# Layer 1's experts: first two gathered by one-hot products, norm's scale and shift on the transposed rows, sixteen weight buffers instead of twelve

## The chip, the core and the metric

The kernel runs on one core of a Trainium2 chip. A core has five engines, each with its own queue of instructions that it works off in the order in which they stand: TensorE (PE in the profile: matrix products, transposes too), VectorE (DVE), ScalarE (ACT), GpSimd (POOL) and SyncE (SP, which here only issues DMAs). Sixteen DMA engines move data between the device's memory and the core's on-chip memory. The metric is the device time of one execution in microseconds (us); less is better.

## The reference

Two layers (`DEPTH = 2`) of a block with four mixers and a mixture of experts run over 256 tokens and, in layer 0, 256 context tokens, each with 1024 numbers. The change concerns the mixture of experts of layer 1 and the norm ahead of it:

```python
def rms_norm(x, g):
    y = x * lax.rsqrt(jnp.mean(x * x, axis=-1, keepdims=True) + EPS)
    return y * g
def modulate(h, shift, scale):
    return h * (1.0 + scale) + shift
...
        x = x + gt1 * (jnp.concatenate([ya, yb, ys, yh], axis=-1) @ w_out[l])
        h2 = modulate(rms_norm(x, norm2_g[l]), sh2, sc2)
        x = x + gt2 * moe(h2, router_w, router_b, moe_w1[l], moe_w3[l], moe_w2[l])
...
def moe(h, w_router, b_router, w1, w3, w2):
    scores = jax.nn.softmax(h @ w_router + b_router, axis=-1)
    # the best of 4 groups of 4 experts, and in it the best 2 experts, with weights that sum to 1
    ...
    for e in range(16):
        he = jax.nn.silu(h @ w1[e]) * (h @ w3[e])
        out = out + gate[..., e:e + 1] * (he @ w2[e])
```

All is in 32-bit floating point. One expert's three matrices have 6 MB, sixteen experts' 96 MB, and each is read once in a layer.

## The kernel before

**The experts.** Routing gives each token's two choices a place in one of the experts' lists. In layer 1 an expert has a list of 64 rows, two of them 128 and 96. What does not fit goes to a loop of extra passes (`extras`, its count `rnx` is computed on the chip; in the run profiled here layer 1 makes no pass). Routing also sorts the experts from the third on by how many tokens they have, so which weights belong to the third, fourth, ... expert is known on the chip alone: `wix` holds the indices, SP reads one into a register (`wdyn`) and issues the loads of that expert's weights (`raw<-in_wmoe_dram`, six of 1 MB each). The first two experts (`STAT = 2`) are fixed, so their loads wait for no routing.

**The norm.** `norm` writes the normed, scaled and shifted rows of each of the two tiles of 128 tokens to a scratch tensor in memory, `h2d`; scale and shift (`a2`, `sh`) are broadcast by DMA to all partitions. GpSimd gathers an expert's rows from it (`xg<-h2d`), PE transposes them (`tp<-cst,xg`), and ACT copies the transposed rows out of the accumulator memory (`ah<-tp`).

**Routing's two halves.** `route` is a generator; its first part gives `p`, the place of each token in each expert's list. `first_slots` turns `p` into the row numbers of the first two experts (`oh`, `rsrc`) and issues their gathers. Then the other parts make `wix`, `rnx` and `rri`, by which GpSimd scatters each token's number and weight into a table in memory (`sld<-rec,rri`, four DMAs) and reads the table back (`rtab<-sld`). From `rtab` come the rows of all later gathers, the weights by which an expert's result is multiplied (`yf<-s,rtab`) and the rows to which it is added (`ybd<-yf,rtab`, a DMA that adds).

**One expert** (`expert32`): products with `w1` and `w3` (both `sc<-raw,ah`, in two accumulators), copies of both by ACT and DVE (`al<-sc`), products with a folding matrix (`tp<-fold,al`), silu on ACT (`al<-tp`), the product on DVE (`ah<-al,tp`), products with `w2` (`mm<-raw,ah`), then `s<-mm`, `s<-s,mm` and `yf<-s,rtab` for each half of the columns. `moe` writes the steps of neighbouring experts interleaved; a scheduler orders each engine's queue when the kernel is built.

**The weights' buffers.** `fetch` puts the 1 MB loads in turn into 12 buffers (7 + 3 + 2), in the order `USE`. A load waits for its buffer's last reader and for the load three ahead of it to have landed (`FLIGHT = 3`). Ahead of the loop over extra passes, which stands between experts 1 and 2, loads are issued until `AHEAD2` of them stand ahead of their use: 21 in all. At the loop each engine waits for every transfer under way.

## Time and profile before

| | |
|---|---|
| median of three runs | 1307.47 us (1305.84 to 1308.94) |
| profiled execution, its own time | 1307.14 us |
| its span, first to last instruction | 1305.1 us, 2.0 us less than its time |
| mean clock granted to TensorE | 0.931 of full speed |
| PE busy | 1146.0 us, 88% of the span |
| DVE, ACT, POOL busy | 731.1, 529.9, 183.9 us |
| loop over extra passes of layer 1 | PE waits for it from 1032.5 to 1042.0 us |

Times in the trace count from the first instruction. Layer 1's experts begin at some 984 us and end at some 1282 us. Since the sum of the busy times mixes stages with different limits, the stage between the norm and the loop has to be read by itself: when each engine works there, and what ends its waits.

### The profile page before, as it was taken

Reading aid. Unit: us, or ns where it says so; the run is one execution under the profiler, and the core shown is the slowest. Engines: PE = TensorE matmul, PEld = TensorE weight load, DVE = VectorE, ACT = ScalarE, POOL = GpSimd, SP = SyncE. Lnnn points to the kernel's source line nnn. Section 1 sums busy time; section 2 is a strip of 40 time slices with the busy share of each in tenths; the row PEclk is TensorE's granted clock in tenths of the full one; section 3 lists DMA queues with packets and bytes.
Section 4 is the critical chain, followed back from the end, with each engine's and each line's share of the span. In section 5 each row is a group of like instructions: output and inputs, shape, how many; then the busy total and the mean of one; then the engine's idle time right before and its main releaser. Section 6 shows DMA issues by size and latency. Waiting matters only on the chain. (4 is left out here: it accounts for less than half of the span.)

```text
span 1305.1 us, 16882 instructions
## 1 busy us (share of the span) xinstructions
PE 1146.0 (88%) x5789; PEld 724.5 (56%) x5789; DVE 731.1 (56%) x1811; ACT 529.9 (41%) x876; POOL 183.9 (14%) x213
## 2 busy tenths in 40 slices
PE   4999999997966799999898799998884499998885
PEld 2677677765855567655454277684771253533332
DVE  6496579788588564455444659599974110101114
ACT  5222642674324464555434452553831122212222
POOL 0200200100044220211100100100102111211102
PEclk9999999896987799999999899999896789999997
DMA  7763752444817798899995743554477699999961
GB/s 298 261 235 135 257 204 86 177 153 158 350 49 258 238 355 319 313 367 387 384 361 183 279 162 131 201 173 162 149 277 314 242 337 396 365 389 388 414 265 65
DMA packets 62009, 334.05 MB, mean 256 GB/s; under 512 B 12217, under 2 KB 13657, under 8 KB 27104
## 3 DMA queue, kind: packets, MB, share of 16 engines
q1 hardware_dynamic: 51840, 313.44, 63.0%
q0 software_dynamic: 10080, 19.50, 5.8%
q8 instruction: 47, 0.77, 0.2%
q14 instruction: 42, 0.34, 0.1%
HBM read 317.51 MB, written 19.15 MB: 258 GB/s over the span
## 5 line engine op out<-in xcount | busy, mean ns | idle before, releaser
L383 DVE TENSOR_TENSOR lo<-raw,hi 128x1024 fp32r<-128x1024 f32 x169 | 203.5, 1222 | 87.4 <-ACT hi L383 82.9
L383 PE MATMUL sc<-raw,ah 128*64 128x512 f32 (+3 forms) x750 | 216.2, 634 | 12.8 <-SPq L2031 9.5
L383 ACT CAST hi<-raw 128x1024 fp32r<-128x1024 f32 x172 | 175.3, 1047 | 116.5 <-PE mm L383 53.6
L383 PEld LDWEIGHTS sc<-raw,ah 128*64 128x64 f32 (+3 forms) x750 | 62.3, 147 | 113.3 <-issue 99.5
L383 PE MATMUL mm<-hi,ah 128*128 128x512 f32 (+3 forms) x264 | 109.1, 415 | 4.4 <-ACT hi L383 4.3
L383 PE MATMUL mm<-lo,ah 128*128 128x512 f32 (+3 forms) x264 | 107.0, 405 | 1.7 <-DVE lo L383 1.6
L383 PE MATMUL mm<-hi,al 128*128 128x512 f32 (+3 forms) x264 | 105.7, 402 | 0.6 <-DVE al L383 0.6
L383 PE MATMUL mm<-raw,ah 128*64 128x512 f32 (+3 forms) x378 | 100.2, 595 | 1.9 <-DVE ah L383 1.9
L383 PE MATMUL mm<-ah,hi 128*128 128x512 f32 (+1 forms) x224 | 88.4, 399 | 1.1 <-DVE ah L383 0.8
L383 PE MATMUL sc<-hi,ah 128*128 128x512 f32 (+3 forms) x176 | 75.8, 432 | 11.5 <-ACT hi L383 6.8
L383 DVE COPY al<-sc 128x512 f32<-128x512 f32 x21 | 14.5, 690 | 126.8 <-PE sc L383 126.8
L383 PE MATMUL mm<-al,hi 128*128 128x512 f32 (+1 forms) x224 | 83.8, 374 | 0.0
L383 PE MATMUL mm<-ah,lo 128*128 128x512 f32 (+1 forms) x224 | 83.2, 372 | 0.0
L383 PE MATMUL ad<-raw,cT 128*32 128x256 f32 (+1 forms) x512 | 67.7, 530 | 11.3 <-DMA raw<-in_wada_dram 8.5
L383 DVE TENSOR_TENSOR s<-s,mm 64x512 f32<-64x512 f32 (+1 forms) x43 | 29.2, 678 | 85.1 <-ACT s L383 85.1
L383 PE MATMUL sc<-lo,ah 128*128 128x512 f32 (+3 forms) x176 | 73.2, 416 | 2.1 <-DVE lo L383 2.1
L383 PE MATMUL sc<-hi,al 128*128 128x512 f32 (+3 forms) x176 | 72.1, 410 | 0.0
L383 PEld LDWEIGHTS tp<-fold,al 128*128 128x128 f32 x336 | 43.0, 201 | 48.9 <-DVE al L383 23.9
L383 PE MATMUL tp<-fold,al 128*128 128x64 f32 x336 | 46.9, 289 | 23.8 <-DVE al L383 14.9
L383 PEld LDWEIGHTS mm<-hi,ah 128*128 128x128 f32 (+3 forms) x264 | 49.4, 188 | 28.3 <-ACT hi L383 6.4
L383 PEld LDWEIGHTS mm<-raw,ah 128*64 128x64 f32 (+3 forms) x378 | 32.7, 142 | 58.3 <-issue 52.0
L383 ACT ACTIVATE al<-tp 128x256 f32<-128x256 f32 x21 | 8.1, 384 | 130.1 <-PE tp L383 130.1
(432 smaller groups left out, 2037.0 us busy)
## 6 DMA issues: line engine op xcount, KB each, us to landing
raw<-in_wmoe_dram SPq DMA_DIRECT2D x192, 1024.0 KB
raw<-in_wada_dram SPq DMA_DIRECT2D x32, 1024.0 KB
raw<-in_win_dram SPq DMA_DIRECT2D x24, 1024.0 KB
raw<-in_wad_dram SPq DMA_DIRECT2D x16, 1024.0 KB
raw<-in_wout_dram SPq DMA_DIRECT2D x8, 1024.0 KB
x<-in_tok_dram SPq DMA_DIRECT2D x8, 512.0 KB
raw<-ybd SPq DMA_DIRECT2D x6, 512.0 KB
slot<-yf SPq DMA_DIRECT2D x36, 64.0 KB
```

What stands on the lines that cost most here:

```text
L383: r = f(*a, **k)
```

## The change

Layer 1 alone is meant. **The norm** writes rows that are only divided by their root mean square (ACT); the broadcasts of scale and shift go, and scale and shift are applied where an expert's rows have been transposed, when each channel is a partition (`shifted`, two DVE operations for 512 columns, in place of ACT's copy). **The first two experts' rows** are no longer gathered by DMA: `first_rows` makes matrices with a row's reciprocal root mean square at its place in the list and zeros elsewhere (`ohf`), and PE multiplies the rows that it has on chip by them, which gathers and transposes at once; ACT applies scale and shift. **The buffers** for weights are 16: four more are made of pairs of half-size tiles (`PARTED`), each filled by two DMAs of 512 KB. The order `SEQ[1]` takes all twelve loads of the first two experts ahead of the third's, and `AHEAD2[1]` is 12, which makes 22 loads ahead of the loop. In both layers the last expert's comparison of row numbers (`rel`) is now issued behind that expert's silu product.

```diff
-    E1=dict(gt=1, a2=1, sh=1, x=2, xs=1, w2=1, t=2),
+    E1=dict(gt=1, x=2, xs=1, w2=1, t=2),
...
+SEQ = [USE, USE[:10] + USE[11:13] + [USE[10]] + USE[13:]]
...
-AHEAD2 = (9, 11)
+AHEAD2 = (9, 12)
+PARTED = (0, 4)
...
+        elif r < n2 + NRAW + n4:
+            t = self.hip.tile([P, 1024], F32, tag="hi", name=nm), self.lop.tile([P, 1024], F32, tag="lo", name=self.nm("raw"))
...
         def norm(i, a):
+            if l == 1:
+
+                for n in range(2):
+                    sl = slice(n * 512, n * 512 + 512)
+                    nc.scalar.activation(xt[i][:, sl], self.x2[i][n], AF.Copy, scale=rs[i])
+                nc.sync.dma_start(self.h2d[l][a * P:(a + 1) * P, :], xt[i])
+                return
...
+    def shifted(self, l, out, x, ks):
+
+        n = len(ks)
+        v = lambda t: t.rearrange("p (k m) -> p k m", k=n)
+        col = lambda part: self.mc[l, part][:, ks[0]:ks[0] + n, 0:1].to_broadcast([P, n, out.shape[-1] // n])
+        self.nc.vector.tensor_tensor(v(out), v(x), col(4), op=ALU.mult)
+        self.nc.vector.tensor_tensor(v(out), v(out), col(3), op=ALU.add)
+
+    def first_rows(self, l):
+
+        nc, rt = self.nc, self.rt
+        ot, m = self.otiles(l), HALF
+        self.first = []
+        for e in range(STAT):
+            ohs = []
+            for a, i in enumerate(ot):
+                oh = self.sx([P, m], "ohf", bufs=4)
+                c = a * 16 + e
+
+                self.first_i = nc.vector.tensor_scalar(oh, self.iota_b[:, 0:m], rt["pos"][:, c:c + 1], self.rs2[i], op0=ALU.is_equal, op1=ALU.mult)
+                ohs.append(oh)
+            pt = self.pstp()
+            for k in range(KB):
+                for a, i in enumerate(ot):
+                    nc.tensor.matmul(pt[:, k * m:(k + 1) * m], lhsT=self.x2[i][k // 4][:, k % 4 * P:(k % 4 + 1) * P], rhs=ohs[a],
+                                     start=(a == 0), stop=(a == len(ot) - 1))
+            t = self.act("ah", F32)
+            for k in range(KB):
+                c = slice(k * m, (k + 1) * m)
+                nc.scalar.activation(t[:, c], pt[:, c], AF.Identity, bias=self.mc[l, 3][:, k, 0:1], scale=self.mc[l, 4][:, k, 0:1])
+            self.first.append([t[:, k * m:(k + 1) * m] for k in range(KB)])
...
-            nc.scalar.copy(t[:, :nb * m], pt[:, :nb * m])
+            if l == 1:
+                self.shifted(l, t[:, :nb * m], pt[:, :nb * m], range(nb * b, nb * b + nb))
+            else:
+                nc.scalar.copy(t[:, :nb * m], pt[:, :nb * m])
...
-            for a in range(NT):
-                nc.vector.tensor_scalar(rel[:m, a:a + 1], rows[:m], 1.0 - 128.0 * a, None, op0=ALU.add)
-                nc.vector.tensor_scalar(self.ohT[:, a], self.iota_b[:m], rel[:m, a:a + 1], None, op0=ALU.is_equal)
+            with self.tc.issue_after(i.ins):
+                for a in range(NT):
+                    nc.vector.tensor_scalar(rel[:m, a:a + 1], rows[:m], 1.0 - 128.0 * a, None, op0=ALU.add)
+                    nc.vector.tensor_scalar(self.ohT[:, a], self.iota_b[:m], rel[:m, a:a + 1], None, op0=ALU.is_equal)
```

The first place where this shows is DVE's queue behind the routing's first part. Before, behind `p` (the places) and the row numbers of the first two experts, there stands all of the routing; `rcnt` begins the part that leads to `wix` and `rri`:

```order
L383 SCALAR_TENSOR_TENSOR p_1928_8931<-tp_8925,Ab_8923 128x32
L383 TENSOR_SCALAR oh_8960<-iota_b,p_1928_8931 128x128
...
L383 TENSOR_SCALAR rsrc_8958<-tp_8959 128x2
L383 TENSOR_SCALAR z_1953_8987<-tp_8959 128x1
...
L383 COPY rcnt_9007<-tp_8928 128x16
...
L383 CAST wix_9033<-rrke_9012 128x14
...
L383 TENSOR_SCALAR rri_9064<-rr_9060 128x4
L383 TENSOR_SCALAR rel_10696<-rtab_9078 64x1 x2
L383 COPY al_9124<-sc_9092 128x512
```

In the changed kernel `al_9127` and `ah_9137` are expert 0's copy and silu product, `s_2009` and `s_2011` the two halves of its result, and `al_9198` is expert 1's copy of its `w3` products:

```order
L386 SCALAR_TENSOR_TENSOR p_1944_8926<-tp_8920,Ab_8918 128x32
L386 TENSOR_SCALAR ohf_8928<-iota_b,p_1944_8926,l20z_8816 128x64
...
L386 COPY al_9127<-sc_9106 128x512
L386 TENSOR_TENSOR ah_9137<-al_9147,tp_9138 128x256
L386 COPY rcnt_9032<-tp_8923 128x16
...
L386 TENSOR_TENSOR s_2009_9157<-s_2009_9157,mm_9152 64x512
...
L386 TENSOR_TENSOR s_2011_9166<-s_2011_9166,mm_9161 64x512
L386 TENSOR_TENSOR rsel_9038<-rrke_9037,cst 128x196
L386 COPY al_9198<-sc_9134 128x512
...
L386 CAST wix_9058<-rrke_9037 128x14
...
L386 TENSOR_SCALAR rri_9089<-rr_9085 128x4
```

So `wix` and `rri` now stand behind the copies and sums that take PE's results of experts 0 and 1; before they stood ahead of all of them, and `rel`, which reads `rtab`, stood between `rri` and the first copy.

The second place is SP's queue. Before, around the two writes of `h2d`, with the load of the last of the first two experts' pieces issued ahead (`raw_8756`) and the third expert's index read behind:

```order
L383 DMA raw_8756<-in_wmoe_dram 128x2048
L383 DMA h2d_221<-x_8572 128x1024
L383 DMA h2d_221<-x_8574 128x512 x2
L2021 TENSOR_LOAD wix_9033
...
L383 DMA raw_2003_9207<-in_wmoe_dram 128x2048
```

and in the changed kernel:

```order
L386 DMA raw_8752<-in_wmoe_dram 128x2048
L386 DMA h2d_221<-x_8572 128x1024
L386 DMA h2d_221<-x_8574 128x1024
L386 DMA raw_9201<-in_wmoe_dram 128x1024
L386 DMA raw_9202<-in_wmoe_dram 128x1024
L386 DMA raw_9205<-in_wmoe_dram 128x1024
L386 DMA raw_9206<-in_wmoe_dram 128x1024
L2050 TENSOR_LOAD wix_9058
```

Two whole loads, as four halves, now follow the writes ahead of the first read of `wix`; behind it stand ten loads up to the loop, where before there were eleven.

The third place is PE's queue where the first two experts begin. Before, `tp_9080` is the transpose of expert 0's gathered rows:

```order
L383 MATMUL tp_8959<-R_8566,oh_8972 128x1
L383 MATMUL tp_9080<-cst,xg_8977 128x64 x8
L383 MATMUL sc_9091<-raw_8642,ah_9089 64x512 x4
```

and in the changed kernel the one-hot products of expert 0, 16 rows of which two stand here, with part of its `w1` products, then those of expert 1:

```order
L386 MATMUL tp_8932<-ohf_8928,yf_6820 128x64
L386 MATMUL tp_8932<-ohf_8930,yf_6821 128x64
...
L386 MATMUL sc_9105<-raw_8638,ah_8949 64x512 x4
L386 MATMUL sc_9105<-raw_8640,ah_8949 64x512
L386 MATMUL tp_8962<-ohf_8958,yf_6820 128x64
L386 MATMUL tp_8962<-ohf_8960,yf_6821 128x64
```

The transposes and the products with `R` are gone, and 32 rows of one-hot products stand in their place, ahead of and between the first products with weights.

## Rows read from the trace of the kernel before

**Rows 1.** Timeline of PE, 971 to 1045 us: start, length, instruction, count, idle before.

```profile
984.37 0.21 PE L383 MATMUL tp<-Ab,ub 128*128 128x32 bf16 x1 [8.11 <-DVE Ab L383]
...
998.38 1.09 PE L383 MATMUL tp<-cst,xg 64*128 64x64 f32 x8 [12.27 <-DVE rext L383]
1000.14 6.90 PE L383 MATMUL sc<-raw,ah 128*64 128x512 f32 x24 [0.68 <-ACT ah L383]
...
1010.33 1.10 PE L383 MATMUL tp<-fold,al 128*128 128x64 f32 x8
1018.42 1.97 PE L383 MATMUL tp<-fold,al 128*128 128x64 f32 x8 [6.99 <-DVE al L383]
...
1042.00 1.98 PE L383 MATMUL sc<-raw,ah 128*64 128x512 f32 x4 [9.50 <-SPq L2031]
```

**Rows 2.** Timeline of DVE, 983 to 1045 us.

```profile
984.63 0.19 DVE L383 SCALAR_TENSOR_TENSOR p<-tp,Ab 128x32 f32<-128x32 f32 x1 [0.32 <-PE tp L383]
...
994.62 0.16 DVE L383 TENSOR_SCALAR z<-tp 128x1 f32<-128x1 f32 x1 [8.31 <-DMA h2d<-x]
...
998.85 0.16 DVE L383 CAST wix<-rrke 128x14 int32<-128x14 f32 x1
...
1002.37 0.17 DVE L383 TENSOR_SCALAR rri<-rr 128x4 int32<-128x4 f32 x1
1017.57 0.21 DVE L383 TENSOR_SCALAR rel<-rtab 64x1 f32<-64x1 int32 x2 [15.03 <-DMA rtab<-sld]
```

**Rows 3.** Timeline of POOL, 996 to 1045 us.

```profile
1002.82 1.04 POOL L383 DMA_INDIRECT sld<-rec,rri  x1 [4.24 <-DVE rri L383]
...
1012.55 0.58 POOL L383 DMA_DIRECT2D rtab<-sld  x1 [4.80 <-DMA sld<-rec,rri]
...
1030.95 1.46 POOL L383 DMA_INDIRECT ybd<-yf,rtab  x1 [10.34 <-ACT yf L383]
```

**Rows 4.** Waits of SP's queue, 999 to 1045 us: total us, times, longest.

```profile
SPq L383 <- PE sc L383: 14.0, 4, 9.4
...
SPq L2031 <- SPq L2031: 7.0, 1, 7.0
```

**Rows 5.** Timeline of SP's queue, 999.5 to 1000.2 us: first load by routing's index.

```profile
999.93 0.36 SPq L383 DMA_DIRECT2D raw<-in_wmoe_dram  x1
```

**Rows 6.** Busy time by stretch: engines' us, granted PE clock, DMA share, GB/s.

```profile
980.00:990.00 10.00, 1.02 (x12) 0.71 (x12) 5.40 (x28) 0.40 (x2) 1.78 (x1) 0.50 1.01 419
...
1000.00:1010.00 10.00, 9.86 (x44) 3.33 (x44) 2.23 (x15) 2.54 (x4) 4.01 (x4) 0.84 0.90 357
...
1040.00:1050.00 10.00, 8.00 (x26) 4.61 (x28) 0.42 (x1) 0.38 (x1) 1.04 (x1) 0.50 0.43 149
...
1060.00:1110.00 50.00, 50.00 (x208) 22.67 (x204) 5.84 (x10) 11.73 (x20) 6.75 (x6) 1.00 1.02 392
```

**Rows 7.** Waits of PE behind the loop, 1042 to 1290 us.

```profile
PE tp L383 <- ACT al L383: 8.6, 7, 1.3
PE tp L383 <- DVE al L383: 5.6, 7, 0.8
```

**Rows 8.** Waits of SP's queue behind the loop, 1049 to 1285 us.

```profile
SPq L383 <- DMA raw<-in_wmoe_dram: 146.7, 67, 4.2
...
SPq L383 <- PE sc L383: 6.3, 7, 4.8
```

**Rows 9.** Timeline of DVE, 974 to 983 us: the norm.

```profile
976.16 1.76 DVE L383 SCALAR_TENSOR_TENSOR l21u<-l21y,l21h 128x1 f32<-128x1 f32 x1
...
982.71 0.68 DVE L383 TENSOR_TENSOR x<-x,sh 128x512 f32<-128x512 f32 x1
```

**Rows 10.** Chain of waits that ended last: start, us, engine, count.

```profile
1054.62 2.63 PE sc L383 x13
```

**Rows 11.** ACT's groups by form, 960 to 1290 us: busy, mean ns, idle before.

```profile
L383 ACT COPY ah<-tp 128x512 f32<-128x512 f32 x17 | 9.8, 584 | 34.8 <-PE tp L383 33.0 <-PE sc L383 1.8
```

**Rows 12.** Groups of all engines, 405 to 450 us (layer 0): ACT at the table.

```profile
L383 ACT ACTIVATE y<-mm,rtab 128x512 f32<-128x512 f32 x2 | 1.4, 687 | 5.6 <-DMA rtab<-sld 5.6
```

More of the change, by code (lines that the diff above doesn't have):

```diff
@@ L532, in pump, with queue @@
             self.lp += 1
-    def queue(self, i):
+    def queue(self, i, more=0):
+        if more:
+            self.flight[-1] = i
+            return
         self.flight.append(i)
@@ L547, in used, with load, fetch @@
         self.pump()
-    def load(self, src):
-        if not self.pre:
-            self.pre.append(self.fetch(src))
-        return self.pre.pop(0)
-    def fetch(self, src):
-        n2, n3 = BUFS[f"R{self.l}"]["raw2"], BUFS[self.scope]["raw3"]
-        r = self.wi % (n2 + n3 + NRAW)
+    def load(self, e, j):
+        while (e, j) not in self.got:
+            self.fetch()
+        return self.got.pop((e, j))
+    def fetch(self):
+        l, key = self.l, SEQ[self.l][self.wi]
+        src = self.source(key[0])(key[1])
+        n2, n3, n4 = BUFS[f"R{l}"]["raw2"], BUFS[self.scope]["raw3"], PARTED[l]
+        r = self.wi % (n2 + NRAW + n4 + n3)
@@ L563, in fetch @@
         else:
             t = self.pg("raw3", 2048)
-        i = self.nc.sync.dma_start(t, src)
-        self.queue(i)
-        if self.wait:
-            self.tc.add_manual_dep(i.ins, self.wait.pop().ins.name, mybir.DependencyInfo(mybir.DependencyClass.Sync, mybir.DependencyReason.DATA),
-                                   reason="first gather first")
-        return t
+        if isinstance(t, tuple):
+            for n, p in enumerate(t):
+                self.queue(self.nc.sync.dma_start(p, src[:, n * 1024:(n + 1) * 1024]), n)
+        else:
+            i = self.nc.sync.dma_start(t, src)
+            self.queue(i)
+            if self.wait:
+                self.tc.add_manual_dep(i.ins, self.wait.pop().ins.name, mybir.DependencyInfo(mybir.DependencyClass.Sync, mybir.DependencyReason.DATA),
+                                       reason="first gather first")
@@ L572, in split, with source @@
+        self.got[key] = t
+    def source(self, e):
+        l = self.l
+        if e not in self.srcs:
+            self.srcs[e] = (self.wdyn(l, self.rt["idx"][0:1, e - STAT:e - STAT + 1]) if e >= STAT
+                            else lambda c: self.I["wmoe"][self.wpos(l, e, c)])
+        return self.srcs[e]
     def split(self, ap, n=1024, after=None, eng=None):
@@ L1875, in first_slots @@
             self.sx([P, n], "r" + tag, dt)
+        if l == 1:
+            self.wait = []
+            self.xgs = [self.pg("xg", D) for j in range(BUFS[self.scope]["xg"])]
+            for t in self.xgs:
+                nc.gpsimd.memset(t, 0.0)
+            return self.first, self.first_i
         src = self.sx([P, STAT], "rsrc", I32)
@@ L1886, in first_slots @@
         self.xgs = [self.pg("xg", D) for j in range(BUFS[self.scope]["xg"])]
-        if l == 0:
-            for _ in range(BUFS[self.scope]["y"]):
-                self.pg("y", D)
+        for _ in range(BUFS[self.scope]["y"]):
+            self.pg("y", D)
         nc.gpsimd.memset(self.xgs[0], 0.0)
@@ L2068, in halves_of, with expert @@
                     yield hi[:, 512:1024], lo[:, 512:1024]
-    def expert(self, l, wsrc, tiles, m, ahead=0, alone=False):
+    def expert(self, l, e, tiles, m, ahead=0, alone=False):
         nc, tc = self.nc, self.tc
@@ L2076, in expert @@
             yo, alone = alone, (self.yring(), self.hilo())
-        ws = self.halves_of(wsrc, alone, ahead)
+        ws = self.halves_of(e, alone, ahead)
         ws = chain([next(ws) for _ in range(2 * ahead)], ws)
@@ L2168, in mm @@
                                             skip_group_check=True, **kw)
-        x = []
+        x = xg if isinstance(xg, list) else []
         nb = 512 // m if G > 1 else 4
-        for b in range(KB // nb):
+        for b in range(0 if x else KB // nb):
             pt = self.pstp()
@@ L2320, in run @@
                     next(route)
+                    if l == 1:
+                        self.first_rows(l)
                     self.last_norm()
                 with self.scoped(f"X{l}"):
-                    self.pre = [self.take("x", l, j) for j in range(self.nahead(l))]
+                    self.got = {SEQ[l][j]: self.take("x", l, j) for j in range(self.nahead(l))}
                     self.cons |= {self.pos["x", l, j] for j in range(BUFS[f"R{l}"]["raw2"], self.nahead(l))}
```

56 lines of the change are left out of this document (29 added, 27 removed).

## The prediction

> **What bounds the kernel now.** I read the stage between the norm and the loop over extra passes first, engine by engine, because the whole change acts there; then what PE and SP wait for behind the loop.
>
> PE's timeline [rows 1] shows the stage from PE's side. The small products that count the routing's places end at some 985 us; then PE does next to nothing until the transposes of expert 0's gathered rows at 998.4, and its first product with weights starts at 1000.1. There is a wait of 7.0 us until 1018.4, for DVE's copy `al`, and one of 9.5 us until 1042.0, put down to SP at the loop. PE had thus ended its part at 1032.5.
>
> DVE's timeline [rows 2] says why. The places `p` are ready at 984.8. DVE then stands 8.3 us until the writes of `h2d` have landed, makes `wix` (done 999.0) and `rri` (done 1002.5) in one go, and stands 15.0 us at `rel`, which needs the table. The copy `al` stands behind `rel`: that is PE's 7.0 us. POOL's timeline [rows 3] gives the table's way: four scatters from 1002.8, 4.8 us of waiting for them, the read of the table issued at 1012.6, and its landing at 1017.6, when `rel` starts. From `rri` to the table it is 1017.57 - 1002.54 = 15.0 us.
>
> What opens the loop is the last weight load. SP's queue waits there 7.0 us for its own last semaphore, and ahead of it 14.0 us in four waits for PE to have read a buffer [rows 4]. The first load by routing's index goes out at 999.9 [rows 5], 0.9 us behind `wix`. So before, routing is early, and the loads come late because the buffers are read late, behind `rel`.
>
> Behind the loop PE is busy for all of 50 us at full clock [rows 6], and its later waits are for copies of ACT and DVE, 14.2 us in all, not for weights [rows 7]. SP's queue there waits 146.7 us for earlier loads to land and 6.3 us for PE to free buffers [rows 8]. So four more buffers can give nothing behind the loop, and what the change is worth is the moment at which PE passes the loop, 1042.0 before.
>
> **The change, step by step.**
>
> *Norm.* Three full-width DVE operations of some 0.7 us and a root step on one column that took 1.76 us [rows 9], where `rel`'s two together take 0.21 [rows 2], stand ahead of `p` on DVE's queue. While it ran, POOL added the shift to the other tile; that addition goes, and I expect the step to fall by some 1.5 us. So 3 x 0.68 + 1.5 = 3.5 us, and `p` is there at 981.3. ACT's new copies could delay the softmax by one copy, 0.6 us [rows 11]; the bounds are 2.9 and 3.5 us of gain, or 1.4 if the root step stays as slow; I keep 3.5.
>
> *One-hot products.* Two comparisons of about 0.2 us each, then 32 matrix instructions of the form that `tp<-fold,al` has (128x64): 8 of those take 1.10 us in one place and 1.97 in another [rows 1], so 4.4 to 7.9 us. The granted clock was 0.50 in this stretch [rows 6], so I take 7.4 for expert 0 and, once PE has been busy, 4.2 for expert 1. ACT's eight small operations follow PE slice by slice; one costs at most what a 512-wide copy does, 0.58 [rows 11]. First product with weights: 981.3 + 0.4 + 7.4 + 0.3 = 989.4 us, 10.7 earlier than now.
>
> *Experts 0 and 1 until the loop.* 16 + 16 + 8 tiles of weights, two instructions each, are 80; 13 take 2.63 us back to back [rows 10], so 16.2 us. With 4.2 for expert 1's one-hot products, 1.1 for the fold and a gap of 0.4 PE ends at 1011.3, where it ended at 1032.5. So far the change gives 21 us.
>
> *The routing behind it.* DVE's new order puts `wix` and `rri` behind expert 1's copy `al_9198`, and that needs PE's last product of this stage: 1011.3 + 0.7 = 1012.0. Now the whole takes 4.4 us from `z` to `wix` and 7.9 to `rri` [rows 2]. About half of the first part (through `rsel`, and the gates) stands ahead of `al_9198`, so some 2.1 and 5.3 us remain, between 0 less and 2.3 more: `wix` at 1014.1, `rri` at 1017.3 (now 999.0 and 1002.5). The routing, alone on DVE before, is 15 us late.
>
> *Loads.* Two static loads land early. Ten stand behind `wix`; 0.9 us later, at 1015.0, the first goes out. Their buffers are free by then, so the stream sets the pace: 1.05 MB at 392 to 419 GB/s [rows 6] is 2.5 to 2.7 us each, 26 for ten, 1.3 until the first bytes; two gathers and one scatter of 0.26 MB share the engines, 0 to 2.5 us. The last lands between 1042.3 and 1045.5. PE restarted 1.3 us after SP's semaphore now (9.5 us of wait, of which SP's 7.0 end at 1040.7), so the loads give 1043.6 to 1046.8.
>
> *Table, gathers, result of expert 0.* `rtab` lands 15.0 us behind `rri`, at 1032.3, gathers of experts 2 and 3 go out, then `ybd` about 3.4 us after the table, at 1035.7. Now `ybd` is issued at 1030.95 and is down before SP's release at 1040.7: at most 9.7 us; a smaller DMA, the table, took 5.0 [rows 2, 3]. I take 8, nearer to the upper end because both scatters move rows while loads run. So 1043.7, and PE at 1045.0 (bounds 1042.0 and 1046.7). The two chains agree: PE passes the loop at 1045.2 where it passed at 1042.0, **3.2 us later**. PE's restart is at half clock now (0.50 in that stretch [rows 6]); I assume the same, though up to 2 us less is possible if the clock comes back sooner.
>
> *Behind the loop.* Per gathered expert two DVE operations of 0.68 us replace ACT's copy of 0.58. DVE stood waiting for PE and ACT for most of that time, and PE's waits for DVE's copy, 0.8 us each [rows 7], come at a point where the shift has already run. I cost it at nothing; if it lay in the way each time, 13 x 1.4 = 18 us would be lost. `rel` moves to the end: 0.2 us.
>
> In layer 0 ACT waits 5.6 us for the same table that `rel` waits for [rows 12], and DVE's next work needs ACT's, so moving `rel` gives nothing there; without ACT's wait it would give up to as much.
>
> *Sum* against the profiled execution's 1307.14 us: + 3.2 + 0.2 = 1310.5 us. The median of the runs is 0.3 us higher than that execution, within what separates runs.
>
> By the page "DMA: Bandwidth & Descriptors" of the Trainium skill (Specifications), reads from memory are limited to about 358 GB/s per core. Ten loads would then take 29.3 us and the loop would open some 3 us later still, near 1314 us. The rows show 392 and 419 GB/s, so the trace disagrees and I use its figure.
>
> **The rivals.**
>
> *No difference.* The loads are not pushed back by gathers and run at the fast end, `ybd` needs 6 us, and the clock returns sooner: PE passes at 1043 and gets 1 to 2 us back: 1307 to 1308. For it speaks that both chains' lower bounds lie there; against it that both must be low together. Also here: the change loses its head start exactly.
>
> *Faster.* The head start of experts 0 and 1 survives: if `wix` and `rri` were made where DVE has nothing to do, between 988 and 999 us, the loads would run from some 1000 with 16 buffers and the loop would open 10 us earlier, at about 1032: 1297 us. It decides whether DVE gets to `rcnt` ahead of PE's results. The printed order speaks against it, since an engine does not overtake in its queue. A smaller form: PE ends its first part well ahead of 1011, each us of which comes off both chains; at 4 us it would be faster than now, 1306 or less.
>
> *Slower by more.* The four transfers in a row (scatters, table, gather, `ybd`) now run while ten loads keep all engines full, where before there were pauses for buffers. If each takes half as long again, 15.0 + 8 becomes 34 us, PE passes at 1056, and it is 1321 us; with a quarter more, 1316. The table's way began with the engines already 0.90 busy [rows 6], so I hold this for less likely. The same page of the Trainium skill (Issuing engines are not separate DMA queues) says that DMAs of all issuing engines run on the same sixteen and interleave, which is this rival; no row here separates the share of it.
>
> **How the numbers follow.** The forecast (1308 to 1314) gets 0.50, no difference 0.20, faster 0.20, slower by more 0.10. A measurement of this kernel tells about 0.2%, 2.6 us, from no change, which is 1310.1 upward; some 0.10 of the forecast lies below that. So slower 0.40 + 0.10 = 0.50, same 0.10 + 0.20 = 0.30, faster 0.20. The range 1300 to 1317 holds the first two cases, half of the faster one (its smaller form) and half of the last, 0.85 in all; the slow bound takes in the upper ends of `ybd` and the loads.
>
> **What would show it.** PE's first product with weights at about 989; PE's last one ahead of the loop at about 1011 and a wait of more than 30 us put down to SP; `wix` behind DVE's second copy, at about 1014; `rri` at 1017 and the table 15 us later; no waits of SP for PE's buffers ahead of the loop; PE's restart at 1045. Wrong would be: PE passing the loop before 1040, waits of PE for DVE behind the loop that grew, or waits for weights there.

## The result and the profile after

| | before | after |
|---|---|---|
| median, run side by side | 1305.01 us (1299.51 to 1308.94, 8 runs) | 1316.28 us (1314.92 to 1319.39, 8 runs) |
| span of the profiled execution | 1305.1 us | 1316.3 us |
| mean clock granted to TensorE | 0.931 | 0.928 |
| DVE busy | 731.1 us | 745.8 us |

The change makes the kernel slower: the ratio is 1.0094, with a 95% interval from 1.0073 to 1.0114, and the medians stand 11.3 us apart. The forecast was 1310.5 us. The two spans stand 11.2 us apart, and three stretches make that up, of which the forecast had one: matched instruction by instruction, layer 0 loses 8.4 us, the stage between the norm and the loop loses 9.8, and what lies behind the loop gains 7.0. These are figures of two single executions; the experiments below show which of them stand in the medians of several.

PE's timeline of the changed kernel (start, length, instruction, count, idle before) answers to [rows 1]:

```profile
988.91 7.06 PE L386 MATMUL tp<-ohf,yf 128*128 128x64 f32 x32 [0.67 <-DVE ohf L386]
...
996.47 5.38 PE L386 MATMUL sc<-raw,ah 128*64 128x512 f32 x10 [0.49 <-ACT ah L386]
1001.78 3.79 PE L386 MATMUL tp<-ohf,yf 128*128 128x64 f32 x32
...
1019.26 4.03 PE L386 MATMUL sc<-raw,ah 128*64 128x512 f32 x17
1054.69 1.09 PE L386 MATMUL tp<-cst,xg 64*128 64x64 f32 x8 [31.41 <-DMA xg<-h2d,rtab]
1060.20 1.98 PE L386 MATMUL sc<-raw,ah 128*64 128x512 f32 x4 [4.42 <-SPq L2060]
```

The one-hot products cost what was forecast (7.06 and 3.79 us for 7.4 and 4.2). PE has ended its part at 1023.29 (1019.26 + 4.03) and then stands 31.4 us for rows that are gathered by the table. DVE's timeline answers to [rows 2]:

```profile
988.23 0.19 DVE L386 SCALAR_TENSOR_TENSOR p<-tp,Ab 128x32 f32<-128x32 f32 x1 [0.32 <-PE tp L386]
...
1010.89 0.69 DVE L386 COPY al<-sc 128x512 f32<-128x512 f32 x1 [19.40 <-PE sc L386]
...
1023.33 0.69 DVE L386 COPY al<-sc 128x512 f32<-128x512 f32 x1 [0.39 <-PE sc L386]
...
1025.85 0.17 DVE L386 CAST wix<-rrke 128x14 int32<-128x14 f32 x1
...
1029.56 0.17 DVE L386 TENSOR_SCALAR rri<-rr 128x4 int32<-128x4 f32 x1
```

DVE stands 19.4 us at the first copy `al`, with all of the routing behind it in its queue. `rri`, 17.7 us behind `p` in [rows 2], is now 41.3 us behind it. POOL's timeline shows the chain that hangs on `rri`, and answers to [rows 3]; ACT's row behind it is the first operation that reads the table:

```profile
1030.55 1.06 POOL L386 DMA_INDIRECT sld<-rec,rri  x1 [28.36 <-DVE rri L386]
...
1040.60 0.58 POOL L386 DMA_DIRECT2D rtab<-sld  x1 [5.13 <-DMA sld<-rec,rri]
1046.28 1.01 POOL L386 DMA_INDIRECT xg<-h2d,rtab  x1 [5.10 <-DMA rtab<-sld]
...
1048.87 1.48 POOL L386 DMA_INDIRECT ybd<-yf,rtab  x1 [0.30 <-issue]
```

```profile
1045.60 1.33 ACT L386 ACTIVATE yf<-s,rtab 64x512 f32<-64x512 f32 x2 [24.03 <-DMA rtab<-sld]
```

SP's queue (waits from 1000 to 1062 us: total, times, longest; to be held against [rows 4]) shows the other chain. The 14.0 us for buffers that PE had to read are gone, and 29.9 us for the routing stand in their place:

```profile
SPq L2050 <- DVE rinc L386: 29.9, 1, 29.9
SPq L386 <- DMA raw<-in_wmoe_dram: 15.3, 7, 2.7
SPq L2060 <- SPq L2060: 9.3, 3, 4.5
```

While SP stands there the DMA engines have nothing to do, and then everything comes at once (busy time by stretch; the last three columns are PE's granted clock, the DMA share and GB/s):

```profile
1010.00:1020.00 10.00, 10.00 (x53) 4.72 (x50) 1.78 (x8) 0.49 (x2) 0.00 (x0) 1.00 0.01 2
...
1040.00:1050.00 10.00, 0.00 (x0) 0.00 (x0) 0.00 (x0) 1.33 (x2) 3.68 (x4) 0.50 1.01 424
```

The page "DMA: Bandwidth & Descriptors" of the Trainium skill (Specifications) gives about 358 GB/s as the limit of a core's traffic with memory, half of what a stack of memory gives to its two cores. Here one core ran, and 424 GB/s over ten microseconds is above that figure, as 392 and 419 in [rows 6] were.

**Layer 0.** The same work, 224 matrix instructions, takes 60 us before and 70 us after; the changed execution came to it 2.0 us ahead, and is 8.4 us behind at its end. First the stretch of the kernel before, then the changed kernel's, then what PE waits for there (600 to 750 us) before and after:

```profile
640.00:700.00 60.00, 53.10 (x224) 26.21 (x222) 29.35 (x31) 28.36 (x38) 4.74 (x3) 0.97 0.91 347
```

```profile
638.00:708.00 70.00, 58.18 (x224) 30.05 (x224) 30.33 (x32) 29.29 (x39) 4.73 (x3) 0.85 0.84 299
```

```profile
PE sc L383 <- ACT hi L383: 3.7, 2, 1.8
...
PE sc L383 <- DVE lo L383: 1.6, 2, 0.8
```

```profile
PE sc L386 <- ACT hi L386: 7.5, 4, 1.9
PE sc L386 <- DVE lo L386: 3.1, 4, 0.8
```

PE waits 5.3 us more for the splits of weights (`hi` on ACT, `lo` on DVE), and the granted clock of the stretch falls from 0.97 to 0.85. ACT's queue says why: at two of layer 0's experts the order has changed, though the change is for layer 1. Here the first of them, before and after:

```
L383 CAST hi_5854<-raw_5852 128x1024
L383 ACTIVATE al_5874<-tp_5865 128x256
L383 CAST hi_5877<-raw_5852 128x1024
L383 COPY ah_5977<-tp_5968 128x512

L386 ACTIVATE al_5874<-tp_5865 128x256
L386 COPY ah_5967<-tp_5958 128x512
L386 CAST hi_5854<-raw_5852 128x1024
L386 CAST hi_5877<-raw_5852 128x1024
```

Before, ACT made one split ahead of the silu step `al`, for which it has to wait for PE, and one behind it; now both splits stand behind that step and the copy `ah`. What the change has in layer 0 beside the place of `rel` is the rewritten `fetch`: `source(e)`, which makes SP read an expert's index, was called when an expert began, and is now called when its first load is issued. Experiment 1 takes that back.

**Behind the loop.** PE's waits from 1062 to 1302 us, which answer to [rows 7], are a little smaller, with one wait less for DVE:

```profile
PE tp L386 <- ACT al L386: 7.3, 7, 1.3
PE tp L386 <- DVE al L386: 4.8, 6, 0.8
```

The rest is clock. From its first stretch at full clock to the last expert's products the mean granted clock is 0.97 before (first fence) and 0.99 after (second): before has four stretches of 3.4 us at half clock, of which the second row shows the first, and after has one. Three stretches fewer are worth some 5.1 us (an estimate: half of 3 x 3.4), and PE's waits are 2.1 us less; together that is the gain of 7.0.

```profile
1170.00:1187.60 17.60, 15.48 (x86) 7.15 (x88) 2.47 (x4) 3.94 (x7) 2.40 (x2) 1.00 1.00 384
1187.60:1191.00 3.40, 3.40 (x12) 0.99 (x8) 0.00 (x0) 0.00 (x0) 0.00 (x0) 0.50 1.02 360
1051.00:1283.00 232.00, 216.68 (x985) 92.34 (x983) 35.87 (x54) 54.88 (x96) 35.53 (x27) 0.97 0.93 357
```

```profile
1070.00:1294.80 224.80, 211.80 (x983) 92.38 (x980) 55.04 (x86) 47.20 (x81) 35.80 (x27) 0.99 0.94 358
```

### The profile page after: what moved, and what is told of

Read it like the earlier page. It is cut to its first block, busy times and chain, and to the rows that moved or that the text cites. A ratio compares the mean times of both kernels' runs of the same rounds, so it can differ in the third digit from the quotient of the medians.

```text
span 1316.3 us, 17027 instructions
## 1 busy us (share of the span) xinstructions
PE 1151.6 (87%) x5829; PEld 734.3 (56%) x5829; DVE 745.8 (57%) x1836; ACT 528.3 (40%) x878; POOL 177.3 (13%) x209
## 5 line engine op out<-in xcount | busy, mean ns | idle before, releaser
L386 PE MATMUL sc<-raw,ah 128*64 128x512 f32 (+3 forms) x750 | 213.0, 618 | 7.2 <-SPq L2060 4.4
L386 PE MATMUL sc<-hi,ah 128*128 128x512 f32 (+3 forms) x176 | 76.9, 438 | 15.9 <-ACT hi L386 11.8
L386 PEld LDWEIGHTS tp<-fold,al 128*128 128x128 f32 x336 | 42.2, 198 | 39.7 <-DVE al L386 15.9
L386 PE MATMUL tp<-cst,xg 64*128 64x64 f32 (+4 forms) x248 | 28.5, 253 | 36.8 <-DMA xg<-h2d,rtab 31.4
```

Of the source, the lines that this page charges most:

```text
L386: r = f(*a, **k)
```

## The experiments

Two theories stood against each other for the stage. One: it loses because the routing is queued on DVE behind copies that wait for PE. The other: it loses because of the loads into the new buffers or the products themselves. Beside them there were layer 0's order and the gain behind the loop to be placed. Each kernel was timed beside the kernel before on one chip; "before" in each ratio is that.

**1. Layer 0's order put back.** The changed kernel, with the index read where it was in layer 0:

```diff
         def begin(e):
+            if l == 0:
+                self.source(e)
```

> The changed kernel, with one line more: in layer 0 alone the read of an expert's index stands again where the expert begins, as in the kernel before, so that the order of layer 0's copies on ACT, DVE and PE is that of before. Theory (layer 0's new order costs time): between 600 and 700 us the changed kernel lost 8 to 10 us against the kernel before; here that loss is gone, and the time is 1306 to 1309 us, ratio to before about 1.002. Rival (the loss in layer 0 is chance, of the two profiled executions): the time stays at 1315 to 1318, ratio 1.009.

Measured: 1309.8 us, ratio 1.0026 (1.0012 to 1.004). PE's waits of 600 to 750 us are those of the kernel before:

```profile
PE sc L386 <- ACT hi L386: 3.7, 2, 1.8
...
PE sc L386 <- DVE lo L386: 1.6, 2, 0.8
```

So some 0.7% of the kernel, 9 us, were lost in a layer that the change had not meant to touch. The result is 0.8 us above the expected range; the rest of the loss stayed.

**2. The routing ahead of the first copies.** The changed kernel, with the two copies `al` of layer 1's first experts held back until `rri` has been issued:

```diff
-        nc.vector.tensor_scalar(ri, r, -float(TT), None, op0=ALU.add)
+        self.ri_i = nc.vector.tensor_scalar(ri, r, -float(TT), None, op0=ALU.add)
...
-            nc.vector.tensor_copy(s3, p3)
+            if l == 1 and e < STAT:
+                with self.tc.issue_after(self.ri_i.ins):
+                    nc.vector.tensor_copy(s3, p3)
+            else:
+                nc.vector.tensor_copy(s3, p3)
```

> The changed kernel, with expert 0's and 1's copies on DVE put behind the routing's last step, nothing else. Theory (the head start is lost because the routing stands behind PE's results of experts 0 and 1): the routing's last step is done at about 998 instead of 1030 us, the table is there at about 1014 instead of 1046, PE passes the loop at 1033 to 1036 instead of 1060, and the time is 1289 to 1294 us, ratio to before 0.99. Rival (the stream of ten loads and the table's transfers set the loop whatever the order): PE passes the loop at 1050 or later and the time is above 1306.

Measured: 1293.4 us, ratio 0.9914 (0.9884 to 0.9944), so 1.8% below the changed kernel, and PE's restart as expected. `rri` came some 5 us later than expected, because DVE stood 5.94 us at `wix` for the writes of `h2d`. DVE's timeline and then PE's:

```profile
985.71 0.19 DVE L386 SCALAR_TENSOR_TENSOR p<-tp,Ab 128x32 f32<-128x32 f32 x1 [0.32 <-PE tp L386]
...
998.44 1.05 DVE L386 CAST wix<-rrke 128x14 int32<-128x14 f32 x1 [5.94 <-DMA h2d<-x]
...
1002.68 0.17 DVE L386 TENSOR_SCALAR rri<-rr 128x4 int32<-128x4 f32 x1
```

```profile
1034.22 1.98 PE L386 MATMUL sc<-raw,ah 128*64 128x512 f32 x4 [4.92 <-SPq L2060]
```

`rri` ends 17.1 us behind `p` instead of 41.5, and PE restarts 26 us earlier. Products, norm, buffers and loads are the same; what differs is the order. It differs in more than the two copies: the silu product `ah` and the two sums `s` follow them on DVE, and PE now does expert 0's `w2` products behind all of expert 1's, where the changed kernel mixed the two. That did not help PE, whose last product ahead of the loop ends 36.3 us behind `p`, against 35.1 in the changed kernel. So the loss of the stage was the order, and in it the place of the routing.

**3. Both.** The changed kernel with the two edits above, the `source(e)` of experiment 1 and the copies held back as in experiment 2.

> The changed kernel with both edits: layer 0's order as before and the routing ahead of the first two experts' copies on DVE. If both theories hold and the two losses add, 1280 to 1286 us, ratio 0.984. If only the routing's place matters, 1289 to 1294; if only layer 0's order matters, 1306 to 1309.

Measured: 1284.61 us, ratio 0.9839 (0.9807 to 0.987). PE restarts at 1025.26. That is as expected: the two repairs add up.

**4. One part alone: the place of `rel`.** The kernel before, with `rel` behind the last expert's silu product (the last hunk of the change):

```diff
-            for a in range(NT):
+            with self.tc.issue_after(i.ins):
+                for a in range(NT):
...
```

> The kernel before, with the last expert's comparison of row numbers issued behind its silu product, as the change has it, and nothing else; the rest of every queue is unchanged. Theory (that comparison held DVE for 15 us at the table and PE for 7 us, and with it the release of weight buffers): PE passes the loop some 5 to 7 us earlier, at 1035 to 1037 us, and the time is 1298 to 1300 us where before is 1305. Rival, as the prediction costed it (0.2 us at the end and no gain): the time stays within 2 us of the kernel before.

Measured: 1298.46 us, ratio 0.9929 (0.9892 to 0.9966). In PE's timeline the 7.0 us ahead of the folding products [rows 1] are gone, and the loop opens 7.1 us earlier, of which 1.0 had been gained ahead of `p` in this execution. So the theory held, and not the prediction's 0.2 us:

```profile
1009.12 2.00 PE L383 MATMUL tp<-fold,al 128*128 128x64 f32 x16
...
1034.90 1.08 PE L383 MATMUL sc<-raw,ah 128*64 128x512 f32 x4 [2.90 <-SPq L2031]
```

**5. One part alone: scale and shift on the transposed rows.** The kernel before, with `norm`, `shifted` and its two uses as in the change:

```diff
+            if l == 1:
+                for n in range(2):
+                    sl = slice(n * 512, n * 512 + 512)
+                    nc.scalar.activation(xt[i][:, sl], self.x2[i][n], AF.Copy, scale=rs[i])
...
-            nc.scalar.copy(t[:, :nb * m], pt[:, :nb * m])
+            if l == 1:
+                self.shifted(l, t[:, :nb * m], pt[:, :nb * m], range(nb * b, nb * b + nb))
```

> The kernel before with one part of the change alone: in layer 1 the norm's scale and shift are put on the transposed rows of every expert by two DVE operations, and the norm itself keeps only the row factor on ACT. Gathers, buffers and the place of rel stay as before, and layer 0 keeps its order. Both theories: the places p come 3.5 to 5 us earlier than before's 984.6 (less layer 0's difference), and with them wix and the loads; since the copy al still stands behind rel, the loop opens 3 to 5 us earlier, near 1038. First theory (the four stretches at half clock behind the loop, which the changed kernel has only one of, go with the two DVE operations per expert): one such stretch, and another 5 us gained behind the loop: 1297 us, 1294 to 1300. Rival (they come from another part of the change): four stretches stay, 1303 us, 1301 to 1306; if PE now waits for DVE's two operations at each gathered expert, 1310 or more.

Measured: 1295.7 us, ratio 0.9924 (0.9888 to 0.9959); a miss in one point of both theories. `p` came 4.8 us earlier than before, with layer 0's 2.2 us taken off, as expected. But the copy `al` of expert 0 did not stay behind `rel`: the scheduler put it ahead, and PE's folding products waited for nothing. The loop opened 4.9 us earlier by the same count, and the remaining 4.7 us of the spans' 11.8 came from behind it, where two stretches at half clock are left of four. That was the first theory's gain there, and PE's waits for DVE did not grow: 5.6 us as in [rows 7].

**6. One part alone: the one-hot products.** The kernel before, with `first_rows` and without the gathers of the first two experts:

```diff
+                    if l == 1:
+                        self.first_rows(l)
...
+        if l == 1:
+            self.wait = []
...
+            return self.first, self.first_i
```

> The kernel before with one part of the change alone: layer 1's first two experts get their rows by one-hot products. The norm writes its scaled and shifted rows as before, and the one-hot result gets scale and shift from ACT; buffers, loads, layer 0's order and the place of rel in the code stay as before. First theory (the loss of the stage is the routing, which DVE's queue now holds behind the copy al of expert 1): wix comes at about 1024 instead of 999, ten loads start behind it, table, gathers and the scatter of expert 0's result are strung behind that, and the loop opens 10 to 16 us later than before; with four stretches at half clock behind the loop as before: 1319 us, 1316 to 1323. Rival (the routing stays in DVE's pauses, and what was lost in the changed kernel came from loads into the new buffers): PE ends its part of the stage 9 us earlier and the loop opens no later than before: 1305 us, 1300 to 1308.

Measured: 1319.54 us, ratio 1.0109 (1.006 to 1.0158). DVE's waits (955 to 1062 us):

```profile
DVE ah L383 <- ACT al L383: 23.3, 2, 20.8
DVE al L383 <- PE sc L383: 18.8, 2, 18.4
DVE rel L383 <- DMA rtab<-sld: 16.0, 1, 16.0
```

This part alone carries the loss of the stage, with the old buffers and the old norm: 18.4 us at the copy `al`, the routing behind it. The loads into new buffers are not needed for it. The loop opens 10.3 us later than before, in an execution whose layer 0 ended 3.8 us earlier: PE restarts 71.5 us behind `p`, 72.0 in the changed kernel and 57.4 before.

**7. One part alone: the buffers.** The kernel before, with sixteen buffers, the new order of loads and one load more ahead of the loop; layer 0's order as before.

```diff
+SEQ = [USE, USE[:10] + USE[11:13] + [USE[10]] + USE[13:]]
...
-AHEAD2 = (9, 11)
+AHEAD2 = (9, 12)
+PARTED = (0, 4)
```

> The kernel before with one part of the change alone: four buffers of layer 1 more (halves of the hi and lo buffers), the changed order of loads, and twelve loads ahead of the loop instead of eleven, with layer 0's order as before. First theory (buffers are not what bounds it: the last load ahead of the loop goes out earlier, but the loop then opens with the scatter of expert 0's result, which stays where rel puts it): SP's waits for PE's buffers ahead of the loop, 14 us, shrink, the loop opens 0 to 2 us earlier, nothing behind it: 1305 us, 1303 to 1307. Rival (the stretches at half clock behind the loop go with the order of loads): another 5 us gained there, 1299 us, 1297 to 1302.

Measured: 1292.77 us, ratio 0.9892 (0.9851 to 0.9934). My theory fell here, and the rival's sum was still too small. SP's waits for buffers that PE had to read shrink (955 to 1062 us; there the kernel before has 19.1 us for `sc`, 14.0 of them in [rows 4], and 7.7 for `mm`):

```profile
SPq L386 <- PE sc L386: 3.3, 2, 3.0
SPq L386 <- PE mm L386: 3.2, 1, 3.2
```

The loop opened 9.7 us earlier, of which layer 0 had brought 4.2 in this execution. Behind it came the remaining 8.8 us of the spans' 18.5, with a mean granted clock of 0.99 as in the changed kernel and the same waits of PE, 7.3 and 4.8 us:

```profile
1040.20:1266.00 225.80, 212.80 (x986) 92.57 (x983) 36.17 (x54) 55.15 (x97) 35.54 (x27) 0.99 0.94 358
```

So the gain of the changed kernel behind the loop comes with the buffers and their order of loads, though weights were not waited for there. The order of PE's products behind the loop changed with them too, and nothing here tells these apart.

**8. The index earlier.** Experiment 3, with `wix` in memory that the norm's rows don't share (a tile allotted early):

```diff
+            self.rt["wixt"] = f([P, NE - STAT], "wix", I32)
...
-        idx = self.rt["idx"] = self.sx([P, nd], "wix", I32)
+        idx = self.rt["idx"] = self.rt["wixt"] if l else self.sx([P, nd], "wix", I32)
```

> The kernel of e3_both with one memory place changed: the tile that wix is written to is allotted early, so that it no longer lies on the norm's rows and no longer waits until these are written out to h2d (5.8 us of DVE's time ahead of wix in e3_both); the order of every queue is the same, and the wait moves to the next operation of DVE that lies on such rows. Theory (loads that start earlier still help, since the last load and the table both end just ahead of the loop): wix some 5 us earlier, the loads with it, PE's restart 1 to 3 us earlier: 1282 us, 1280 to 1284. Rival (the table's way alone sets the restart, and rri has not moved): 1284.6 us, within 1 us of e3_both.

Measured: 1283.46 us, ratio 0.9813 (0.9773 to 0.9853); not to be told from experiment 3, and so neither theory is decided by the time. `wix` ended 6.9 us behind `p` instead of 13.6, `rri` 15.1 instead of 17.0, and PE restarted 47.9 us behind `p` instead of 48.6: 0.7 us for loads that could start 6.7 us earlier.

**9. The one-hot part left out.** Experiment 1 with `first_slots` as before, so that the first two experts are gathered by address:

```diff
-                    if l == 1:
-                        self.first_rows(l)
...
-            return self.first, self.first_i
```

> The changed kernel with one part undone, the one-hot products (the first two experts' rows are gathered by address as before), and with layer 0's order as before; norm, buffers and the place of rel stay changed. First theory (the one-hot products give the loop nothing, since PE has slack ahead of it; the routing, now at its old place, the loads and the table set it): p at 977 to 980, rri 21 us behind it as in e5_norm_only, ybd 20 us behind rri as in e4_rel_late, PE's restart 5 to 8 us behind ybd's issue, at 1024 to 1029, and behind the loop one stretch at half clock: 1284 to 1288 us, no more than 0.3% from e3_both. Rival (the gathers by address, which PE waits for until some 994, hold PE, so that expert 0's result and its scatter come later than the table): the restart stays at 1032 to 1035 as in e5_norm_only and e7_buffers_only: 1292 to 1296 us.

Measured: 1290.72 us, ratio 0.9872 (0.9839 to 0.9905). Neither: PE restarted at 1032.95, as late as the rival said, but not for its reason, since expert 0's scatter was issued at 1018.67 and PE then stood for later transfers. Stretches of this kernel, and then of experiment 3 (`p` at 977.3 and 976.6 us):

```profile
990.00:995.00 5.00, 1.08 (x8) 0.92 (x8) 5.00 (x35) 0.00 (x0) 2.99 (x3) 0.50 0.17 49
```

```profile
990.00:995.00 5.00, 5.00 (x40) 4.08 (x42) 3.24 (x22) 1.25 (x5) 0.77 (x2) 1.00 0.94 318
```

The first of the two is this kernel's: its DMA engines pause, where loads wait for the first gather, and PE does little; in experiment 3 both work.

**10. Two parts that each gained.** The edits of experiments 4 and 7 together, on the kernel before:

> The kernel before with two parts of the change, the buffers with their order of loads and the place of rel; norm and gathers as before, layer 0's order as before. First theory (in e7_buffers_only the scatter of expert 0's result set the loop, because the copy al stood 8.1 us behind rel): with rel late ybd is issued 20 us behind rri, 9 us earlier than there, and the loop opens 5 to 8 us earlier than in e7_buffers_only, at 1024 to 1028: 1285 us, 1283 to 1289. Rival (the loads set it by then, and rel gains nothing once the buffers are there): the loop opens at 1031 to 1033: 1291 to 1294 us.

Measured: 1289.84 us, ratio 0.987 (0.9844 to 0.9896), and PE restarts at 1032.17, as the rival said; the time lies between the two ranges. With the buffers there, the 0.7% of `rel` is worth no more than the two intervals can tell from nothing. Each of them takes away the same wait, that of SP's loads for buffers that PE has to read: from 955 to 1062 us it was 26.8 us before, 11.2 in experiment 4, 6.5 in experiment 7 and 1.0 here.

**11. Experiment 9 without the wait for the first gather.**

```diff
+        if l == 1:
+            self.wait = []
         return xg, i
```

> The kernel of e9_without_onehot with one wait less: in layer 1 the next load of weights no longer waits until the first gathered rows have landed. There SP's queue stood 12.1 us for that gather and the DMA engines were 0.17 busy from 990 to 995 us, where in e3_both they were 0.94 busy; the order of every queue stays. First theory (the loads set the loop in e9_without_onehot, and what the one-hot products are worth is the loads' start that no longer waits for a gather): the loads fill that gap, the last one ahead of the loop lands 3 to 6 us earlier than there, PE restarts at 1027 to 1030, and it is 1285 to 1288 us. Rival (the gathers, now behind loads on the same DMA engines, come that much later and with them PE's first products and expert 0's result): 1290 us or more, PE's first product with weights at 1001 or later.

Measured: 1290.28 us, ratio 0.9893 (0.9862 to 0.9924). The gap was filled:

```profile
990.00:995.00 5.00, 0.00 (x0) 0.00 (x0) 1.16 (x11) 0.00 (x0) 1.40 (x2) 0.50 1.03 404
```

Yet the time is the same, and it is the rival's, though not for its reason: behind `p`, PE's products came no later. PE's first product with weights came 20.7 us behind `p` (20.8 in experiment 9), `rri` 22.6 (21.5), and the restart 55.0 (55.7). So the theory fell that this pause was what the one-hot products save. The profile alone would mislead here: PE restarted at full clock (1.00 from 1036.8 to 1050 us, where experiment 9 has 0.65 from 1033 to 1046), and what lies behind took 4.4 us less; but the execution had come to `p` 4.5 us later, and the medians agree.

**12. No step of the routing waits for the norm's rows.** Experiment 8 with four more tiles allotted early:

```diff
+            self.rt["XTt"], self.rt["qt"], self.rt["rt"] = f([P, 2, 2, NT], "XT", F32), f([P, 2, NT], "q", F32), f([P, 2, NT], "r", F32)
+            self.rt["rit"] = f([P, 2, NT], "ri", I32)
```

> The kernel of e8_both_early_index with four more small tiles (those from rXT to rri) allotted early, so that no step of the routing waits any more until the norm's rows are written out to h2d; the order of every queue is the same. In eleven of the kernels run so far PE restarts 30 to 36 us behind the end of rri, whatever wix does. First theory (rri, with the scatters, the table and expert 0's scatter behind it, sets the loop): rri loses the wait of 4.4 us and ends 10.5 to 11 us behind p instead of 15.1, PE restarts 3 to 4.5 us earlier with respect to p, and it is 1279.5 us, 1278 to 1282. Rival (the ten loads set it by now: they begin at wix, which has not moved): the restart stays 47 to 48 us behind p and it is 1283 us, within 1.5 us of e8_both_early_index.

Measured: 1283.5 us, ratio 0.9823 (0.9786 to 0.986): the rival. `rri` ends 10.6 us behind `p`, as expected, and PE restarts 49.0 us behind `p`, no earlier than in experiment 8. So the end of `rri` alone does not set the restart. The stretches of this kernel show what is left:

```profile
985.00:995.00 10.00, 9.51 (x44) 5.96 (x44) 3.45 (x23) 2.47 (x8) 4.12 (x5) 0.67 1.01 396
995.00:1005.00 10.00, 10.00 (x51) 4.19 (x52) 0.69 (x1) 4.23 (x10) 2.38 (x3) 1.00 1.02 388
1005.00:1015.00 10.00, 8.57 (x44) 3.03 (x38) 1.79 (x3) 1.96 (x4) 1.97 (x2) 1.00 1.00 362
```

The DMA engines are full from 985 us until the loop is near; moving the routing once more gained nothing. That full DMA engines set the restart now is the likely reading; no run here gives them less to do. Experiments 3, 8 and 12 are one result, 1.6 to 1.9% below the kernel before and the best that was run.

## Why the prediction was right in direction and wrong in size

**The stage: the mechanism was right, four terms were too small.** The routing behind expert 1's copy, the empty DMA engines, PE's long wait for SP and the table were forecast, and experiments 2 and 6 show that they are the cause. With layer 0's 8.4 us taken off, the changed kernel against the forecast:

| step | forecast | measured less 8.4 | off by, in this step |
|---|---|---|---|
| `p` ready | 981.3 | 980.0 | -1.3 |
| PE ends its part ahead of the loop | 1011.3 | 1014.9 | +4.9 |
| `wix` done | 1014.1 | 1017.6 | -0.1 |
| `rri` done | 1017.3 | 1021.3 | +0.5 |
| `rtab` landed (start of the first operation that reads it) | 1032.3 | 1037.2 | +0.9 |
| PE past the loop | 1045.2 | 1051.8 | +1.7 |

The largest is PE's: I counted 80 weight products at full clock behind a stretch whose clock the rows gave as 0.50, and ten of them ran at half clock, 5.38 us where thirteen take 2.63 in [rows 10]. That is 3.4 of the 4.9 us. I had given the low clock to expert 0's one-hot products alone. Another 0.9 is the folding products: there are 16 in this stage [rows 1], and the sum priced 8. The last step is the loads and the scatter `ybd`: from its issue to PE's restart it was 11.3 us, where the sum had 9.3. The norm erred the other way: `p` gained 4.8 us, here and in experiment 5, where the sum had 3.5. Five full-width DVE operations go ahead of `p`, from 974.0 to 983.4 us in the kernel before, and I counted three.

**Layer 0: the step that failed.** The prediction took layer 0 into account only for `rel`, and costed it at nothing. It cost 8.4 us in the profile and 0.7% in experiment 1. Experiment 1 shows what it was: the call that reads an expert's index had moved, and with it ACT's splits of weights at two experts. The printed orders of the two kernels had it; the prediction used them only where the change was meant to act.

**Behind the loop: wrong sign.** "I cost it at nothing" and `rel`'s 0.2 us gave +0.2; measured were -7.0. The two DVE operations per expert were indeed hidden, but I did not ask what a changed order does to the clock. I took "full clock" from the first 50 us behind the loop; further on the kernel before already showed less:

```profile
1160.00:1210.00 50.00, 45.09 (x205) 17.96 (x203) 4.94 (x8) 10.42 (x18) 8.16 (x7) 0.93 1.01 387
```

Counted from PE's restart to the end of the span, experiment 7 gives 8.8 us with the buffers alone, experiment 5 4.7 with the norm alone, experiment 4 1.1 with `rel`; these do not add up to the 7.0. What decides whether a stretch at half clock comes is left open: each order showed its own number of them in its profile, and no run here changes one pause of PE alone. It is not chance of an execution: all ten profiled kernels with the sixteen buffers have one such stretch, 150 us (157 in experiment 11) behind the first moment at full clock, and the two with twelve buffers and the old norm and gathers, the kernel before and experiment 4, have four, the first after 136.5 us.

**Four more buffers "can give nothing behind the loop", and what they give ahead of it:** the first half was wrong, as said. SP's waits for PE to free buffers there were 11.1 us, not the 6.3 of [rows 8], which leaves out 4.5 for `mm` and 0.3 for `tp`; in the changed kernel they are 5.1. In the second, I had put the late loads down to `rel`, and rightly (experiment 4), but did not see that the buffers by themselves lift the same wait (experiment 7).

**The net hid large terms.** The errors in layer 0 and behind the loop, +8.4 and -7.2, nearly cancel; with the stage's +6.6 they make the 7.8 us by which the profiled execution, 11.2 us above that of before, missed the +3.4 forecast.

**The rivals.** *Faster* was described by its mechanism: routing made where DVE has nothing to do. It did not come about, since the order was against it; when experiment 2 brings it about, the time is 1293.4 us where the rival said 1297. *Slower by more*, with all four transfers a quarter longer, gave 1316, which is the time measured, but by luck: from `rri` to the table it was 15.9 us instead of 15.0, and from `ybd`'s issue to the restart 11.3 instead of 9.3, so 2.9 us in all, half of the 5.8 that the rival needs; the rest of the loss was layer 0's and PE's. *No difference* needed both chains at their lower ends; PE passed at 1051.8 by the count above, beyond the upper end of both.

**What stays open.** Why the one-hot products gain beside a repaired order. The twelve runs with them (experiments 3, 8 and 12) took 1281.6 to 1287.6 us, the eight without them (9 and 11) 1286.9 to 1295.9. The ratios are 0.981 to 0.984 against 0.987 and 0.989: some single intervals overlap, but together a difference of some 0.6% is clear of the noise. The two groups differ in one thing more, the copies `al` that are held back in the first. The profiles put the restart 6 to 8 us earlier behind `p` with the one-hot products, and by experiment 11 the pause of the DMA engines is not the reason.

## What to carry to other kernels

When work moves to an engine that a later stage waits for, look at what stands behind it in that engine's queue: here a copy that waited 19.4 us for PE held all of the routing, and holding two copies back until the routing was issued was worth 1.8%. Compare the printed order on all engines over the whole program, also in parts that the change does not mean to touch: a function called later had moved the splits of weights at two experts of layer 0, for 0.7%. Parts that gain by themselves need not add up, where they lift the same wait (`rel` 0.7%, buffers 1.1%, both together 1.3%).

## What was not expected of the hardware

Behind the loop PE's clock fell to half for 3.4 us at a time although PE was busy for 15.48 of the 17.6 us ahead of it (1170.0 to 1187.6, above), with waits of at most 1.3 us; the kernel before had four such stretches and the changed one a single one, with PE's waits smaller by only 2.1 us in sum.

Some operations of DVE beside a running operation of POOL ended only with it, and others took their usual time (seen, not tried by itself). `wix`, 0.17 us in the changed kernel, took 1.05 in experiment 2 and ended at 999.49, 0.03 us behind POOL's clearing of a tile of 128x1024 (first fence). The norm's root step took 1.76 us [rows 9] and ended at 977.92, 0.01 us behind POOL's addition in the kernel before (second fence):

```profile
998.50 0.96 POOL L386 MEMSET xg<- 128x1024 f32 x1 [0.30 <-DMA h2d<-x]
```

```profile
975.57 2.34 POOL L383 TENSOR_TENSOR x<-x,sh 128x1024 f32<-128x1024 f32 x1 [37.15 <-DVE l2s L383]
```

In the changed kernel, which has no such addition, the step took 0.22 us:

```profile
983.34 0.22 DVE L386 SCALAR_TENSOR_TENSOR l21u<-l21y,l21h 128x1 f32<-128x1 f32 x1
```

But in the kernel before, the six DVE operations that ran beside a clearing of the same size (996.33 to 997.31 us) took 0.15 to 0.51 us each, as elsewhere. Which operations are held is left open.
